# One-core two-block network: modulation products held back in stretches, score trees started one by one, input squares on ScalarE

## The chip, the cores and the metric

One core of one Trainium2 chip runs the whole program in one launch. The metric is the device time of an execution in microseconds (us), taken as the median of several runs. The engines are TensorE (PE; its weight loads are listed as PEld), VectorE (DVE), ScalarE (ACT), GpSimd (POOL) and SyncE (SP, which only issues DMAs). Each executes its own instructions in one order that is fixed before the launch.

## The reference, cut to what matters

Two networks of two layers run one after the other on a sequence of 512 vectors of width 1024, in fp32.

```python
# first network, x: 512 x 1024
x = x + even_mixer(rms(x))      # retention (4 heads) and HGRN2 (4 heads), gates, output product
x = x + memory_attention(x)     # 256 memory vectors
x = x + conv_ffn(x)
x = x + odd_mixer(rms(x))       # 8 heads of dilated attention, biases by distance
x = x + memory_attention(x)
x = x + conv_ffn(x)
# second network, context ctx: 256 x 1024
for i in range(2):
    mod = silu(c) @ ada_w[i] + ada_b[i]        # six vectors of 1024 out of 1024 x 6144 weights
    mod_c = silu(c_ctx) @ ada_w[i] + ada_b[i]
    h, hc = modulate(rms(x), mod), modulate(rms(ctx), mod_c)
    x, ctx = x + g * mixer(h, hc), ...
    x, ctx = x + g * swiglu(modulate(rms(x))), ...
out = rms(x)
```

`modulate(x, shift, scale)` is `x * (1 + scale) + shift`. The vectors `mod` and `mod_c` depend on `c`, `c_ctx` and weights alone, so that they can be computed any time before the second network needs them.

## The kernel before, in words

**Weight products.** Activations lie feature-major: 8 tiles of 128 features x 512 positions. A weight unit (128 x 1024, 512 KB) is loaded by SP into one of 4 buffers (`raw`), rounded to the matmul type by ACT (`wh`, L293), and its rest is taken by DVE (`wl`, L294). A product of one unit is 24 matmuls of 128x512 into one PSUM tile: wh by the high and the low part of the activation, and wl by the high part (`fm`, L312; `fm2_step`, L342; `fm1`, L939; `dx`, L1158; time-major forms `tm`, L357, `tm_c`, L1183, and `tm_dual`, L1202). `split` (L401 to L405) makes the two parts of an activation, with one ACT and one DVE instruction.

**Statistics.** `stat_add` squares a new tile on ACT (L423) and adds it on POOL, the last of eight on DVE (L428). `stat_end` sums over features with matmuls by a column (`colsum`, L417) and POOL takes the power -1/2 (L411). `bcast` brings the result to all partitions with four transposes on PE (L480). In the even mixer, which is the first stage, POOL both squares the eight input tiles (L513) and adds the squares (L515). `head_part` (L459, L460 on DVE) and `head_rstd` (L442 on PE) do the same for one head.

**Modulation products.** `ada(l, j)` computes vector j of layer l outside TensorE. For each of 2 halves and 8 row blocks it loads a 128x512 weight tile with SP (256 KB, L1053, two steps ahead) and adds it, scaled by one scalar per partition, to an accumulator on DVE (L1060, L1062; two instructions a step where both `mod` and `mod_c` are wanted, otherwise one). Then DVE transposes and sums (L1066, L1068), and PE adds up (L442). It is a generator: each step ends in a `yield`. The generator `side` chains all twelve vectors, with four empty turns first. `tick` advances it by one turn, and is called at the start of each weight product `fm`, `fm1`, each of `fm2_start`, and each `wt`. In layer 0 each step takes two turns, in layer 1 one. `finish_side` runs the rest at once, where the second network starts.

**Order.** The tile framework orders each engine's instructions at build time: of those it takes to be ready, it takes the one that stands first in the program, so that the program text acts as a list of priorities. `weave` writes such a text: it keeps up to `depth` generators active, takes one step of each in a round, and then runs `rate` background jobs a round.

**Stages that the change touches.** `even_mixer` projects the inputs of the HGRN2 heads (`hg_inputs`, L565 to L579), then builds the scores of four heads as trees (`tree`, L581): at each of seven levels four PE products (L591), one merge and three scalings on DVE (L609 to L622), each waiting for the level before. The trees are woven with the value products, the retention inputs and the retention heads. `odd_mixer` projects queries and keys of a head in three steps (`project`, L963) and weaves attention with the further projections and the memory keys and values of the next stage. `conv_ffn` writes its output in three passes of eight blocks; the last pass also makes the next stage's split and statistics. `ab_mixer`, the first stage of the second network, weaves the three steps of `modulate` (statistics, broadcast, the eight tiles) between the four units of the context's value product.

Of the kernel before, what the change touches and what calls it, by code (L numbers as in the profile page):

```python
# [10 lines left out]
AF = mybir.ActivationFunctionType  # L11
ALU = mybir.AluOpType
# [213 lines left out]
class Net:  # L226
    def __init__(self, ctx, tc, a):
        self.tc, self.nc, self.a = tc, tc.nc, a
        E = ctx.enter_context
        self.cp = E(tc.tile_pool(name="cp", bufs=1))  # L230
        self.xp = E(tc.tile_pool(name="xp", bufs=9))
        self.cx = E(tc.tile_pool(name="cx", bufs=9))
        self.A = E(tc.tile_pool(name="A", bufs=NSLOT))
        self.sp = E(tc.tile_pool(name="sp", bufs=40))
        self.wr = E(tc.tile_pool(name="wr", bufs=4))
        self.wh = E(tc.tile_pool(name="wh", bufs=3))
        self.wl = E(tc.tile_pool(name="wl", bufs=3))
        self.pm = E(tc.tile_pool(name="pm", bufs=4, space=PSUM))
        self.pa = E(tc.tile_pool(name="pa", bufs=4, space=PSUM))
        self.dp = E(tc.tile_pool(name="dp", bufs=1, space=bass.MemoryType.DRAM))  # L240
        self.n = 0
        self.side = None
        self.early = []
        self.consts()

# [114 lines left out]
            evac(tb, pss[tb])  # L360

    def tick(self):
        if self.side is not None and next(self.side, None) is None:
            self.side = None

    @staticmethod
    def weave(units, bg=(), depth=4, rate=1.0):

        units, bg, active, due = iter(units), iter(bg), [], 0.0
        while True:  # L370
            while len(active) < depth:
                u = next(units, None)
                if u is None:
                    break
                active.append(u)
            if not active:
                break
            for g in list(active):
                if next(g, "end") == "end":
                    active.remove(g)  # L380
            due += rate
            while due >= 1.0:
                due -= 1.0
                job = next(bg, None)
                if job is not None:
                    job()
        for job in bg:
            job()
# [115 lines left out]
    def even_mixer(self, x, filler):  # L504
        nc, a = self.nc, self.a
# [3 lines left out]
        for k in range(8):  # L509
            xs.append(self.split(x[k], scale=self.V("mixg0", k)))  # L510
            self.fm2_step(first, xs, k)
            sq = acc if k == 0 else self.T()
            nc.gpsimd.tensor_tensor(sq, x[k], x[k], ALU.mult)  # L513
            if k:
                nc.gpsimd.tensor_tensor(acc, acc, sq, ALU.add)  # L515
        first = [[ps for ps, _ in first], [self.fm("w_ev", 17, xs)]]
        rstd, _ = self.stat_end([acc])
# [9 lines left out]
        mx = self.S(4)  # L527
# [37 lines left out]
        def hg_inputs(h):  # L565
            pf, pq = first[h] if h < 2 else (self.fm("w_ev", 16 + h, xs), None)
            th = self.T()
            nc.vector.tensor_mul(th, pf, rb)
            nc.scalar.activation(th, th, AF.Tanh, scale=0.5)
            f = self.T()  # L570
            nc.vector.tensor_scalar(f, th, fa[:, h:h + 1], fb[:, h:h + 1], ALU.mult, ALU.add)
            KS = self.T()
            nc.gpsimd.tensor_scalar(KS, f, -1.0, 1.0, ALU.mult, ALU.add)
            nc.vector.tensor_scalar(f, f, 1e-6, None, ALU.max)
            if pq is None:
                pq = self.fm("w_ev", 12 + h, xs)
            QP = self.T()
            nc.vector.tensor_mul(QP, pq, rb)
            return QP, KS, f  # L579
# [128 lines left out]
            ys[h] = self.split(o)  # L708

        hv, rv, sc, ri, gates = [], [], {}, {}, {}  # L710
        inp = {0: hg_inputs(0)}
        self.mem_prep()

        def trees():
            for h in range(4):
                if h not in inp:
                    inp[h] = hg_inputs(h)
                yield tree(h, *inp[h])
# [12 lines left out]
        jobs = [next_inputs] * 3  # L731
        jobs += [lambda: self.tm("w_evt", 1, xs, v_evac(hv, False)), lambda: self.tm("w_evt", 0, xs, v_evac(rv, True))]
        jobs += [lambda: ret_in(0), lambda: ret_in(1)]
        for h in range(4):
            jobs.append(lambda h=h: retention(h, *ri[h]))
            if h < 2:
                jobs.append(lambda h=h: ret_in(h + 2))
        self.weave(trees(), jobs, depth=4, rate=0.75)
        extra = []
        jobs = iter(filler(extra))  # L740
        for h in range(8):
# [148 lines left out]
    def conv_ffn(self, l, x, st, xs, gain=None, mid=None):  # L890
        nc = self.nc
        first = self.fm2(f"w_fi{l}", (0, 22), xs)
        rstd, _ = self.stat_end(st)
        hid = []
        third = self.fm(f"w_fi{l}", 1, xs)
        rb = self.bcast_sb(rstd)

        def gate_up(j):
            pg, pu = first if j == 0 else (third if j == 1 else self.fm(f"w_fi{l}", j, xs), None)
            g, y = self.T(), self.T()  # L900
            nc.vector.tensor_mul(g, pg, rb)
            nc.scalar.activation(y, g, AF.Identity, bias=self.V(f"cb{l}", j), scale=self.V(f"cw{l}", 44 + j))
            nc.vector.scalar_tensor_tensor(y[:, 1:512], g[:, 0:511], self.V(f"cw{l}", 22 + j), y[:, 1:512], ALU.mult, ALU.add)
            nc.vector.scalar_tensor_tensor(y[:, 2:512], g[:, 0:510], self.V(f"cw{l}", j), y[:, 2:512], ALU.mult, ALU.add)
            nc.scalar.activation(y, y, AF.Gelu_apprx_tanh)  # L905
            nc.gpsimd.tensor_tensor(y, y, rb, ALU.mult)  # L906
            if pu is None:
                pu = self.fm(f"w_fi{l}", 22 + j, xs)
            nc.vector.tensor_mul(y, pu, y)
            hid.append(self.split(y))  # L910

        for p, (lo, hi) in enumerate(PARTS):
            for j in range(len(hid), min(hi + 1, 22)):
                gate_up(j)
            out, st, nxt = [], [], []
            for m in range(8):
                if mid is not None and p > 0:
                    next(mid, None)
                ps = self.fm1(f"w_fo{l}", m * 3 + p, hid[lo:hi])
                t = self.xp.tile([128, 512], F32, tag="x", name=f"x{self.n}")  # L920
                nc.vector.tensor_add(t, ps, x[m])
                out.append(t)
                if p == 2:
                    if gain is not None:
                        nxt.append(self.split(t, scale=self.V(gain, m)))
                    self.stat_add(st, m, t)
            x = out
        return x, st, nxt

    def fm1(self, w, u, xs, n=512):  # L930
# [12 lines left out]
    def odd_mixer(self, x, st, xs, filler):  # L943
# [19 lines left out]
        def project(h):  # L963
            q, k, sq, sk = self.T(), self.T(), self.T(), self.T()
            tb = self.T()
            nc.scalar.dma_start(tb, self.a["odb"][h])
            nc.gpsimd.tensor_tensor(tb, tb, odm, ALU.add)
            pk = self.fm("w_od", 8 + h, xs)
            nc.scalar.copy(k, pk)
            nc.scalar.activation(sk, pk, AF.Square)  # L970
            sk = self.head_part(sk)
            yield
            pq = self.fm("w_od", h, xs)
            nc.scalar.copy(q, pq)
            nc.scalar.activation(sq, pq, AF.Square)
            sq = self.head_part(sq)
            rk = self.head_rstd(sk, 128, xv)
            yield
            rq = self.head_rstd(sq, 128, xv)
            pb = self.bcast(rk)  # L980
            nc.vector.scalar_tensor_tensor(k, k, gqk[:, 0:1], pb, ALU.mult, ALU.mult)
            p[h] = q, k, rq, tb
# [26 lines left out]

        pj = [project(h) for h in range(8)]  # L1010
        extra = []
        for h in (0, 0, 1, 0, 1):
            next(pj[h], None)
        values(1)
        next(pj[1], None)

        def units():
            for h in range(8):
                self.run(pj[h])
                ys.append((self.T(F32R), self.T(F32R)))  # L1020
                for i in range(4):
                    yield attend(h, i, *p[h])

        jobs = [lambda h=h: next(pj[h], None) for h in range(2, 8) for _ in range(3)]
        ff = filler(extra)
        jobs = jobs[:12] + ff[:1] + jobs[12:17] + ff[1:3] + jobs[17:] + ff[3:]
        self.weave(units(), jobs, depth=3, rate=0.85)
        return self.residual("w_odo", ys, x, "xag1"), extra


# [216 lines left out]
    def ab_mixer(self, x, st, c, cs):  # L1247
# [47 lines left out]
                nc.gpsimd.tensor_tensor(t[:, 0:w], t[:, 0:w], u[:, 0:w], ALU.mult)  # L1295
                ys.append(self.split(t) if n == 4 else self.split_c(t))

        for _ in self.tm_c("w_abt", 1, cs, ev_n):
            next(mx, None)
        self.run(mx)  # L1300
        self.tm_dual("w_abt", 1, xs, None, ev_n)
        win = [[], [], [], []]
# [578 lines left out]
def body(ctx, tc, a, stop=None, start=None):  # L1881
# [32 lines left out]
    def side(ls):  # L1914
        if start in (None, "mix0"):
            for _ in range(4):
                yield True
            k.ada_prep()
        for l in ls:
            for j in range(6):  # L1920
                for _ in k.ada(l, j):
                    for _ in range(2 - l):
                        yield True

    def finish_side(l):
        while (l, 5) not in k.done:
# [76 lines left out]
```

## Time and profile before

| | |
|---|---|
| median of 3 runs | 3152.65 us (3144.85 to 3153.3) |
| the profiled execution's own time | 3151.23 us |
| its span, first to last instruction | 3149.4 us |
| PE busy | 3091.8 us, 98% of the span, 16292 matmuls |
| PEld busy | 2587.4 us, 82% |
| DVE busy | 1779.6 us, 57% |
| ACT busy | 1118.9 us, 36% |
| POOL busy | 437.8 us, 14% |
| DMA | 312.79 MB, 99 GB/s |

The shares are averages over stages with different limits. [...] A wait is the idle time of an engine before an instruction, and is put down to the instruction that ended last. Matmul ends are modelled: a matmul that is listed with 0.39 us can be followed by the next one 0.23 us after its start.

### The profile page before, as it was taken

How to read it: one execution, taken by the hardware profiler on the slowest of the kernel's cores; microseconds unless marked ns; L12 is line 12 of the kernel's file. 1: busy time of each engine (PE TensorE's matmuls, PEld its weight loads, DVE VectorE, ACT ScalarE, POOL GpSimd, SP SyncE). 2: the span in 40 equal slices, each digit the busy share in tenths (PEclk: the TensorE clock that was granted, in tenths of full speed). 3: DMA queues.
4: the chain of work that ended last, by engine and by line, in shares of the span. 5: the costliest groups of instructions: out<-in, count | busy, mean ns of one | idle time of the engine just before them, and what ended most of it. 6: DMA issues, size and time to landing. Idle time of an engine off the chain costs nothing. (4 is left out here: it accounts for less than half of the span.)

```text
span 3149.4 us, 40994 instructions
## 1 busy us (share of the span) xinstructions
PE 3091.8 (98%) x16292; PEld 2587.4 (82%) x16292; DVE 1779.6 (57%) x2894; ACT 1118.9 (36%) x1859; POOL 437.8 (14%) x375
## 2 busy tenths in 40 slices
PE   8999999999999999999999999999999999999998
PEld 6878888888877888888878778888888878888887
DVE  7867676565658767768663567343322453543333
ACT  2224353232435544423343545211212352342222
POOL 5023111010111111102021113000000320110001
PEclk9999999999999999999999999999999999999999
DMA  5224323333333423334342012332211221123222
GB/s 170 75 80 154 117 78 119 115 127 117 125 103 103 147 84 106 119 128 153 131 150 96 29 36 103 107 113 72 88 67 53 69 99 37 39 100 99 95 97 71
DMA packets 110354, 312.79 MB, mean 99 GB/s; under 512 B 12177, under 2 KB 17682, under 8 KB 110162
## 3 DMA queue, kind: packets, MB, share of 16 engines
q1 hardware_dynamic: 101968, 297.32, 28.0%
q10 hardware_dynamic: 8194, 12.86, 1.3%
q8 instruction: 128, 2.10, 0.3%
q14 instruction: 64, 0.52, 0.1%
HBM read 306.98 MB, written 3.15 MB: 98 GB/s over the span
## 5 line engine op out<-in xcount | busy, mean ns | idle before, releaser
L1158 PE MATMUL m<-t,wh 128*128 128x512 f32 (+1 forms) x4124 | 1092.1, 352 | 1.1 <-DVE t L1110 0.4
L293 ACT CAST wh<-wr 128x1024 fp32r<-128x1024 f32 (+2 forms) x485 | 488.0, 1008 | 1241.8 <-PE m L1158 419.3
L294 DVE TENSOR_TENSOR wl<-wr,wh 128x1024 fp32r<-128x1024 f32 (+2 forms) x485 | 579.3, 1195 | 453.3 <-ACT wh L293 442.0
L1158 PEld LDWEIGHTS m<-t,wh 128*128 128x128 f32 x4124 | 726.1, 190 | 114.9 <-issue 11.5
L312 PE MATMUL m<-t,wh 128*128 128x512 f32 (+1 forms) x2576 | 772.4, 382 | 0.0
L1158 PE MATMUL m<-t,wl 128*128 128x512 f32 (+1 forms) x2062 | 723.9, 351 | 0.5 <-DVE wl L294 0.5
L312 PEld LDWEIGHTS m<-t,wh 128*128 128x128 f32 x2576 | 473.9, 188 | 89.5 <-issue 1.0
L312 PE MATMUL m<-t,wl 128*128 128x512 f32 (+1 forms) x1288 | 491.1, 381 | 0.2 <-DVE wl L294 0.2
L1158 PEld LDWEIGHTS m<-t,wl 128*128 128x128 f32 x2062 | 390.6, 189 | 53.1 <-issue 1.9
L312 PEld LDWEIGHTS m<-t,wl 128*128 128x128 f32 x1288 | 242.7, 188 | 46.9 <-issue 0.7
L428 POOL TENSOR_TENSOR t<-t,t 128x512 f32<-128x512 f32 (+1 forms) x90 | 116.0, 1295 | 1163.0 <-ACT t L423 1162.7
L1062 DVE SCALAR_TENSOR_TENSOR t<-t,silc,t 128x512 f32<-128x512 f32 x280 | 219.5, 812 | 15.5 <-DMA t<-w_ada 14.9
L939 PE MATMUL m<-t,wh 128*128 128x512 f32 x704 | 217.2, 390 | 0.0
L342 PE MATMUL m<-t,wh 128*128 128x512 f32 x496 | 159.4, 401 | 7.3 <-ACT wh L293 7.3
L939 PEld LDWEIGHTS m<-t,wh 128*128 128x128 f32 x704 | 131.9, 188 | 27.2
L906 POOL TENSOR_TENSOR t<-t,t 128x512 f32<-128x512 f32 x44 | 64.8, 1473 | 549.6 <-ACT t L905 539.9
L401 ACT CAST t<-t 128x512 fp32r<-128x512 f32 x116 | 72.0, 621 | 189.6 <-DVE t L1520 104.0
L939 PE MATMUL m<-t,wl 128*128 128x512 f32 x352 | 136.9, 389 | 0.0
L1428 DVE SCALAR_TENSOR_TENSOR x<-m,modt,x 128x512 f32<-128x512 f32 (+1 forms) x70 | 49.3, 704 | 154.2 <-PE m L1158 154.2
L411 POOL TENSOR_TENSOR s<-s,nh 128x4 f32<-128x4 f32 (+2 forms) x67 | 72.3, 1081 | 429.9 <-DVE s L473 155.7
L357 PE MATMUL m<-wh,t 128*128 128x512 f32 x384 | 123.4, 397 | 0.0
L342 PEld LDWEIGHTS m<-t,wh 128*128 128x128 f32 x496 | 93.6, 192 | 26.3 <-ACT wh L293 7.3
(387 smaller groups left out, 3384.5 us busy)
## 6 DMA issues: line engine op xcount, KB each, us to landing
t<-w_ada SPq DMA_DIRECT2D x192, 256.0 KB, 4.1
wr<-w_fi SPq DMA_DIRECT2D x88, 512.0 KB, 3.3
wr<-w_gu SPq DMA_DIRECT2D x88, 512.0 KB, 3.2
wr<-w_fo SPq DMA_DIRECT2D x32, 512.0 KB, 3.4
wr<-w_dn SPq DMA_DIRECT2D x32, 512.0 KB, 3.3
wr<-w_ev SPq DMA_DIRECT2D x24, 512.0 KB, 3.2
wr<-w_xk SPq DMA_DIRECT2D x16, 512.0 KB, 3.4
wr<-w_xv SPq DMA_DIRECT2D x16, 512.0 KB, 3.2
```

The source lines that it names most:

```text
L293: nc.scalar.copy(h[:, 0:e], r[:, 0:e])
L294: nc.vector.tensor_sub(lo[:, 0:e], r[:, 0:e], h[:, 0:e])
L312: nc.tensor.matmul(ps[:, 0:n], A[:, s], B[:, 0:n], start=c == 0, stop=c == tot - 1)
L342: self.nc.tensor.matmul(ps, A[:, s], B, start=k == 0 and i == 0, stop=k == K - 1 and i == 2)
L357: nc.tensor.matmul(pss[tb], A[:, ts], B[:, s], start=(u == 0 and j == 0 and i == 0), stop=(u == nu - 1 and j == kper - 1 and i == 2))
L401: nc.scalar.copy(h[:, 0:n], src[:, 0:n])
L411: self.nc.gpsimd.tensor_tensor(r, v, self.nh[:, 0:w], ALU.pow)
L428: e.tensor_tensor(st[0][:, 0:n], st[0][:, 0:n], sq[:, 0:n], ALU.add)
L906: nc.gpsimd.tensor_tensor(y, y, rb, ALU.mult)
L939: nc.tensor.matmul(ps[:, 0:n], A[:, s], B[:, 0:n], start=c == 0, stop=c == tot - 1)
L1062: nc.vector.scalar_tensor_tensor(acc[i], r, s, acc[i], ALU.mult, ALU.add)
L1158: nc.tensor.matmul(ps[:, s], A[:, ws], B[:, s], start=j == 0 and i == 0, stop=j == last and i == 2)
```

## The change

While a new flag `quiet` is set, `tick` does nothing. It is set over the tree weave of the even mixer, over the weave of the odd mixer, and in the last pass of `conv_ffn` over the last four blocks. The layer-0 steps of `side` take one turn instead of two. `weave` gets an argument `ramp`: in round r at most 1 + r // ramp generators are active; the trees use ramp 2. The squares of the even mixer's input tiles go from POOL to ACT. The odd mixer's `project` has four steps instead of three, its key scale's sum comes a step later, and the job list and rate are fitted to that. In `ab_mixer`, `modulate` is advanced after the second and the fourth unit instead of after each.

```diff
@@ class Net, __init__
+        self.quiet = False
@@ tick
-        if self.side is not None and next(self.side, None) is None:
+        if self.side is not None and not self.quiet and next(self.side, None) is None:
             self.side = None
@@ weave
-    def weave(units, bg=(), depth=4, rate=1.0):
+    def weave(units, bg=(), depth=4, rate=1.0, ramp=None):
-        units, bg, active, due = iter(units), iter(bg), [], 0.0
+        units, bg, active, due, r = iter(units), iter(bg), [], 0.0, 0
         while True:
-            while len(active) < depth:
+            top = depth if ramp is None else min(depth, 1 + r // ramp)
+            r += 1
+            while len(active) < top:
@@ even_mixer
-            nc.gpsimd.tensor_tensor(sq, x[k], x[k], ALU.mult)
+            nc.scalar.activation(sq, x[k], AF.Square)
...
+        self.quiet = True
         inp = {0: hg_inputs(0)}
         self.mem_prep()
...
-        self.weave(trees(), jobs, depth=4, rate=0.75)
+        self.weave(trees(), jobs, depth=4, rate=0.75, ramp=2)
+        self.quiet = False
@@ conv_ffn
+                self.quiet = p == 2 and m > 3
                 ps = self.fm1(f"w_fo{l}", m * 3 + p, hid[lo:hi])
...
+        self.quiet = False
         return x, st, nxt
@@ odd_mixer, project
             sq = self.head_part(sq)
+            yield
             rk = self.head_rstd(sk, 128, xv)
-            yield
             rq = self.head_rstd(sq, 128, xv)
+            yield
             pb = self.bcast(rk)
@@ odd_mixer
-        for h in (0, 0, 1, 0, 1):
+        for h in (0, 0, 1, 0, 1, 0):
             next(pj[h], None)
         values(1)
-        next(pj[1], None)
+        for h in (1, 1):
+            next(pj[h], None)
+        self.quiet = True
...
-        jobs = [lambda h=h: next(pj[h], None) for h in range(2, 8) for _ in range(3)]
+        jobs = [lambda h=h: next(pj[h], None) for h in range(2, 8) for _ in range(4)]
         ff = filler(extra)
-        jobs = jobs[:12] + ff[:1] + jobs[12:17] + ff[1:3] + jobs[17:] + ff[3:]
-        self.weave(units(), jobs, depth=3, rate=0.85)
+        jobs = jobs[:16] + ff[:1] + jobs[16:23] + ff[1:3] + jobs[23:] + ff[3:]
+        self.weave(units(), jobs, depth=3, rate=1.05)
+        self.quiet = False
@@ ab_mixer
-        for _ in self.tm_c("w_abt", 1, cs, ev_n):
-            next(mx, None)
+        for i, _ in enumerate(self.tm_c("w_abt", 1, cs, ev_n)):
+            if i in (1, 3):
+                next(mx, None)
         self.run(mx)
@@ body, side
                 for _ in k.ada(l, j):
-                    for _ in range(2 - l):
-                        yield True
+                    yield True
```

## Rows read from the trace of the kernel before

**Rows 1.** The page's busy times: engine, busy us, share of the span, instructions.
```profile
PE 3091.8 (98%) x16292; PEld 2587.4 (82%) x16292; DVE 1779.6 (57%) x2894; ACT 1118.9 (36%) x1859; POOL 437.8 (14%) x375
```

**Rows 2.** PE's waits over the span: total us, times, longest us.
```profile
PE a L417 <- DVE t L428: 11.3, 6, 2.5
...
PE a L591 <- DVE t L578: 3.0, 1, 3.0
PE a L442 <- DVE s L460: 3.0, 3, 2.2
PE m L342 <- DVE wl L294: 2.4, 2, 1.2
...
PE a L635 <- DVE t L632: 1.3, 1, 1.3
PE a L417 <- POOL t L515: 1.2, 1, 1.2
```

**Rows 3.** Busy us (instructions) by stretch: PE, PEld, DVE, ACT, POOL; PEclk, DMA share, GB/s.
```profile
0.00:40.00 40.00, 28.97 (x108) 22.12 (x109) 27.22 (x33) 15.61 (x21) 25.87 (x20) 0.96 0.68 231
...
60.00:80.00 20.00, 16.72 (x100) 15.45 (x99) 19.39 (x37) 1.57 (x2) 1.12 (x2) 0.83 0.27 93
80.00:240.00 160.00, 158.41 (x882) 128.97 (x882) 114.20 (x225) 42.20 (x58) 25.32 (x16) 1.00 0.23 76
240.00:440.00 200.00, 197.37 (x1157) 167.06 (x1156) 142.81 (x232) 92.67 (x164) 44.95 (x33) 1.00 0.36 119
440.00:840.00 400.00, 400.00 (x1792) 330.99 (x1792) 262.88 (x337) 142.36 (x178) 53.68 (x35) 1.00 0.36 121
...
950.00:970.00 20.00, 17.82 (x103) 13.70 (x102) 15.81 (x34) 7.16 (x18) 4.50 (x4) 0.91 0.29 96
...
1600.00:1630.00 30.00, 26.35 (x106) 20.84 (x105) 22.44 (x27) 14.41 (x19) 9.86 (x6) 0.89 0.53 176
```

**Rows 4.** The instructions of lines 513, 515 and 423: duration ns min/median/max, first and last start.
```profile
L513 POOL TENSOR_TENSOR t<-xin x8: 1040/1486/2024, 4.8 to 28.1; 128x512 f32<-128x512 f32 x8
L515 POOL TENSOR_TENSOR t<-t,t x7: 1265/1627/2157, 8.7 to 30.2; 128x512 f32<-128x512 f32 x7
L423 ACT ACTIVATE t<-x x96: 400/617/635, 328.3 to 3139.1; 128x512 f32<-128x512 f32 x64, 128x256 f32<-128x256 f32 x32
```

**Rows 5.** Timeline, DVE's rest of the weights with POOL busy, then idle: start, us.
```profile
7.61 2.06 DVE L294 TENSOR_TENSOR wl<-wr,wh 128x1024 fp32r<-128x1024 f32 x1
...
54.06 1.22 DVE L294 TENSOR_TENSOR wl<-wr,wh 128x1024 fp32r<-128x1024 f32 x1
```

**Rows 6.** Timeline where the trees begin: start, us; idle time before and its releaser in brackets.
```profile
53.72 0.43 DVE L574 TENSOR_SCALAR t<-t 128x512 f32<-128x512 f32 x1 [3.98 <-POOL t L573]
...
66.15 0.74 DVE L1062 SCALAR_TENSOR_TENSOR t<-t,silc,t 128x512 f32<-128x512 f32 x1
...
67.64 2.04 PE L591 MATMUL a<-t,t 128*128 128x128 f32 x8 [2.99 <-DVE t L578]
```

**Rows 7.** Timeline in the odd mixer's weave.
```profile
956.93 2.45 DVE L1062 SCALAR_TENSOR_TENSOR t<-t,silc,t 128x512 f32<-128x512 f32 x2 [1.65 <-DMA t<-w_ada]
...
961.11 0.25 PE L442 MATMUL a<-s,fold 128*32 128x4 f32 x8 [2.18 <-DVE s L460]
```

**Rows 8.** Timeline where the second network begins.
```profile
1605.58 2.57 DVE L1062 SCALAR_TENSOR_TENSOR t<-t,silc,t 128x512 f32<-128x512 f32 x2
...
1610.36 1.80 PE L417 MATMUL a<-c,t 128*128 128x1 f32 x8 [2.48 <-DVE t L428]
...
1617.26 0.60 PE L480 MATMUL a<-ident,s 128*128 128x128 f32 x4
...
1624.90 0.50 PE L1202 MATMUL m<-wh,t 128*128 128x512 f32 x1 [1.10 <-DVE t L1110]
```

**Rows 9.** DVE's waits for the modulation weights: total us, times, longest us.
```profile
DVE t L1062 <- DMA t<-w_ada: 14.9, 13, 4.3
```

**Rows 10.** Line 1062 alone by stretch: DVE busy us (instructions), PEclk, DMA share, GB/s.
```profile
240.00:440.00 200.00, 21.23 (x28) 1.00 0.36 119
440.00:840.00 400.00, 50.67 (x66) 1.00 0.36 121
```

More of the change, by code (lines that the diff above doesn't have):

```diff
@@ L976, in project @@
             sq = self.head_part(sq)
+            yield
             rk = self.head_rstd(sk, 128, xv)
+            rq = self.head_rstd(sq, 128, xv)
             yield
-            rq = self.head_rstd(sq, 128, xv)
             pb = self.bcast(rk)
```

## The prediction

> **What bounds the kernel now.** First the page's busy times: PE is busy for 98% of the span, DVE for 57% [rows 1]. The 440 to 840 us stretch shows what that means: PE without a gap, 1792 matmuls in 400 us, 223 ns each, and so 24 x 0.223 = 5.4 us for one weight unit [rows 3]. The change takes no matmul away. All that it can win is PE's idle time, 3149.4 - 3091.8 = 57.6 us, and what PE loses while its clock is granted at 0.5. So I read second PE's waits [rows 2], then the stretches around the edits with their clock [rows 3], and last the timeline at each wait [rows 5 to 8]. The reader is to see there that after a wait of 2 to 3 us the clock falls for some microseconds: 0.83 over 60 to 80 us, 0.91 over 950 to 970, 0.89 over 1600 to 1630, against 1.00 in stretches without such a wait [rows 3]. A stretch loses about (1 - PEclk) x its length on top of the wait.
>
> **Input squares by ACT.** POOL does 8 squares of 1.49 us and 7 additions of 1.63 us, the last starting at 30.2 us [rows 4], and PE then waits 1.2 us for the sum [rows 2]. Without the squares POOL has 7 x 1.63 = 11.4 us left, so the sum is done before PE has finished its three products: this wait goes. DVE also gains. Its rest of a weight unit took 2.06 us beside POOL and 1.22 alone [rows 5], and PE waited 2 x 1.2 us for just these two instructions [rows 2]; 0.84 us less in each saves 1.7 of 2.4 us, of which I count 1.5. The mean clock of the first 40 us, 0.96, is 1.6 us lost [rows 3]; I count half as won, 0.8. ACT gets 8 x 0.62 = 4.9 us [rows 4] and has 40 - 15.6 = 24.4 us free in that stretch [rows 3]; the work is hidden unless the squares are put ahead of the splits that PE waits for, where each costs up to 0.62 us. Sum 1.2 + 1.5 + 0.8 = **3.5 us won**, bounds -4.9 (every square in the way) and 1.2 + 2.4 + 1.6 = 5.2.
> [...]
>
> **Trees.** At 64.65 us PE waits 3.0 us for the last head's inputs (L578), behind a DVE that has stood 3.98 us for POOL and then did modulation products [rows 6]. With its clock the stretch loses 3.0 + 0.17 x 20 = 6.4 us [rows 3]; from 80 to 240 us another 1.6 us are idle, 1.3 of them at L635 [rows 2, 3]. The text before makes all four heads' inputs before the first tree step, and rounds 1 to 3 then hold only empty jobs. With ramp 2 the trees begin in rounds 0, 2, 4 and 6, so heads 2 and 3 are projected (four units, 21 us of PE) while trees 0 and 1 run; the weave has 17 rounds instead of 11, so all but one of its 13 jobs stand beside trees. The 12 units in it no longer tick: 6 steps, some 9 us of DVE at two times 0.75 us [rows 6], leave the one stage where DVE works 114.2 of 160 us and 19.4 of 20 [rows 3]. POOL, free sooner, has the memory's squares done before the heads' keys need it. What is late next is the last tree alone: its levels follow one another with less beside them. I leave one wait like L635's, 1.3 us, and 1.2 for it: 8.0 - 2.5 = **5.5 us won**, bounds -3 (a wait like L578's comes back in a second place) and 8.0.
>
> **Odd mixer.** PE's 2.2 us wait for L460 came of DVE's order: DVE stood 1.65 us for a modulation tile, did two products in 2.45 us, and only then the head's sums [rows 7]. With the clock, 0.09 x 20 = 1.8, that is 4.0 us [rows 3]. Quiet takes those products out, and the extra step puts a weight unit (5.4 us) between a head's sums and the matmul that needs them. The job list keeps pace: 24 + 15 jobs at 1.05 a round are 37 rounds, 18 + 15 at 0.85 were 39. Small waits in the same weave may give 0.5. **4.5 us won**, bounds 0 and 4.8.
>
> **Start of the second network.** The last residual block's sum was held up on DVE by two products of 2.57 us, and PE waited 2.48 us [rows 8]. Quiet alone takes that away, and the statistics standing after the second context unit (2.7 us later) cover it twice. With the clock, 0.11 x 30 = 3.3, the loss is 5.8, plus 1.1 at the first product that reads the modulated tiles: 6.9 us. But the broadcast now stands behind the fourth unit. Before, it began at 1617.26 and PE could pass its last wait at 1624.90, 7.6 us later, with 5.5 us of context units between [rows 8]. Now nothing lies between. Bounds for the new wait: the same chain, 7.6 - 0.6 = 7.0 us, or, with DVE and ACT free, the broadcast's followers alone, some 3 to 4 us (two DVE, two ACT instructions and one of POOL, 0.6 to 1.5 each, by the kinds in [rows 4 to 6]). The clock then falls as after the other waits, 1.8 to 3.4. I take 4 + 2.4 = 6.4: **0.5 us won**, bounds 6.9 - 10.4 = -3.5 and 6.9 - 4.8 = 2.1. The quiet end of the first conv_ffn has no wait of note: 0.
>
> **Denser products elsewhere.** Turns before: 4 + 192 + 96; now 4 + 96 + 96. Units that tick: 28 in the first stage (24 after the trees, 4 ahead of them), 16, 64, 12, 16, 64, together 200, so all vectors are ready when the first network ends, layer 0 after 104 units. Before, layer 0 needed most of the second conv_ffn and layer 1 reached into the second network; there DVE is relieved, where it bounds nothing: 0. In 440 to 840 us there were 66 products in 50.7 us [rows 10]; now about 64 steps of two, 128, so +62 x 0.77 = 48 us, and some 10 for four more halves' transposes. DVE goes from 262.9 to about 320 of 400 us [rows 3, 10], 80%, hidden behind PE by weights prepared up to three units ahead. From 240 to 440 us there are 28 products [rows 10], 48 with each unit ticking: +15 us on 142.8 of 200 [rows 3]. The tiles are loaded two steps ahead, which is now two units (11 us) instead of four. DVE waited 14.9 us for them in 13 places [rows 9], and of these PE felt the one in rows 7. I count **1.5 us lost**, bounds 0 and 24 (six waits such as that one, 4.0 each).
>
> **Sum.** 3.5 + 5.5 + 4.5 + 0.5 - 1.5 = 12.5 us. The profiled execution took 3151.2 us, near the 3152.7 median of the runs, so I subtract from 3151.2: **3139 us**, 0.4% less. A measurement of this kernel can tell 0.3%, 9.5 us, from no change; faster means below about 3143.
>
> **The rivals.**
> *The waits only move.* For: the broadcast without cover is plain in the text; the trees' last levels have little beside them. Then the second network's start gives -3.5, the trees 2, the rest as above: 3.5 + 2 + 4.5 - 3.5 - 1.5 = 5, 3146 us, no change. Against: the two units behind the old broadcast did not prevent the old wait either, so the chain has slack to lose. Chance 0.26.
> *Denser products bind DVE.* DVE executes in order, so that each late modulation tile or POOL instruction holds up the weights' rests behind it. The place is 240 to 440 us and the first conv_ffn's last pass, where products, splits and POOL's additions meet; the price is 4.0 us a wait; from the fourth wait on (14 + 1.5 against 4 x 4.0) the gain is gone, and at six it is 3151.2 - 14 + 24 = 3161 us, slower. For: half the lead for the tiles. Against: 80% load and three units of stock. Chance 0.10.
> *All touched waits vanish*, at the upper bounds: 5.2 + 8.0 + 4.8 + 2.1 = 20, 3131 us. The second start speaks against it. Chance 0.10.
>
> **How the numbers follow.** The forecast has 0.54, with a range of its own from 3132 to 3147 (each term half way to its bounds), of which about 0.45 lie below 3143. Faster: 0.45 + 0.10 = 0.55. Within 0.3%: 0.09 + 0.25 = 0.34. Slower: 0.11. The range for 8 in 10 takes in the moved waits whole and most of the high gain: 3125 to 3155.
>
> **What would show it.** In the new profile: no wait at L342 for wl above 0.5 us and none at L417 for POOL; no wait of 3 us at L591, PEclk 1.00 over the trees; no wait at L442 in the odd weave, and no L1062 there; at the second network's start no wait at L417 but one of 3 us or more at L1202 or at the tiles' makers; no L1062 after the first network. Wrong would be new waits of over 2 us between 240 and 840 us, or an L1062 ahead of a late L294 there; or a PE as idle as before with the waits at other lines.

## The result, and the profile after

The changed kernel takes 3166.28 us (median of 5 runs, 3164.23 to 3168.97) against 3149.13 of the kernel before on the same chip: ratio 1.0061, interval 1.0050 to 1.0073 (that of the two medians is 1.0054). It is slower by 17 us; the forecast was 3139 us. The profiled execution of after took 3168.89 us, its span 3167.1, so that the spans of before and after (3149.4) differ by 17.7 us. In after.py the lines stand 1 to 12 lines lower: L294 is now L295, L312 L313, L405 L409, L442 L446, L591 L595, L939 L947, L1062 L1074, L1202 L1214.

First the page's busy times of after, to be read beside [rows 1]:

```profile
PE 3097.7 (98%) x16292; PEld 2588.0 (82%) x16292; DVE 1781.4 (56%) x2894; ACT 1121.4 (35%) x1867; POOL 423.9 (13%) x367
```

PE has the same 16292 matmuls. It idles 69.4 us instead of 57.6, and its matmuls take 5.9 us more: the loss is new waits and the clock behind them. Where it lies is read from the first and last start of lines that mark the ends of stages (view of one line; first and last start are the two numbers ahead of the forms). Before:

```profile
L648 PE MATMUL a<-t,t x32: 272/275/275, 213.5 to 240.4; 128*128 128x128 f32 x32
L939 PE MATMUL m<-t,wh x704: 387/389/499, 577.7 to 1604.5; 128*128 128x512 f32 x176
```

After, the same two lines (the trees' last outputs; the products of `conv_ffn`'s last pass in both blocks):

```profile
L652 PE MATMUL a<-t,t x32: 272/275/275, 214.3 to 243.0; 128*128 128x128 f32 x32
L947 PE MATMUL m<-t,wh x704: 387/389/502, 598.0 to 1627.5; 128*128 128x512 f32 x176
```

With the first score of the odd mixer (908.4 before, 932.0 after) and the first product of the modulated tiles (1623.2, 1643.5) the span falls into six stretches:

| stretch | before | after | won | forecast |
|---|---|---|---|---|
| start to the last tree output | 240.4 | 243.0 | -2.6 | 3.5 + 5.5 |
| to the first product of the first `conv_ffn`'s last pass | 337.3 | 355.0 | -17.7 | -1.5 for these two |
| to the odd mixer's first score | 330.7 | 334.0 | -3.3 | |
| to the second `conv_ffn`'s last product | 696.1 | 695.5 | 0.6 | 4.5 |
| to the first product of the modulated tiles | 18.7 | 16.0 | 2.7 | 0.5 |
| to the end | 1526.2 | 1523.6 | 2.6 | 0 |

The second row is as large as the whole loss; the others cancel. That stretch by itself, before (PE, PEld, DVE, ACT, POOL busy us and instructions; PEclk, which is the mean granted TensorE clock as a share of full speed, DMA share, GB/s, as in [rows 3]):

```profile
240.43:577.74 337.31, 334.68 (x1779) 280.65 (x1778) 239.25 (x358) 148.39 (x238) 69.48 (x49) 1.00 0.36 120
```

After, with two pieces of it:

```profile
460.00:475.00 15.00, 11.80 (x40) 8.96 (x39) 12.69 (x16) 3.69 (x6) 3.51 (x2) 0.77 0.37 123
540.00:555.00 15.00, 11.25 (x50) 8.81 (x50) 13.10 (x21) 4.36 (x6) 1.48 (x1) 0.89 0.49 170
242.98:598.01 355.03, 342.35 (x1788) 285.46 (x1786) 276.92 (x416) 147.71 (x237) 67.42 (x48) 0.98 0.39 132
```

PE idled 2.6 us there before and idles 12.7 now; the clock, 0.98 of 355 us, gives about 7: 10.1 + 7.1 = 17.2 of the 17.7 us. DVE has 37.7 us more to do and is still only 78% busy, but 13.10 of 15 us around one of the waits. Line 1074 alone, by stretch, beside [rows 10] (instructions 28 to 47, 66 to 126, as forecast):

```profile
240.00:440.00 200.00, 35.57 (x47) 0.99 0.41 138
440.00:840.00 400.00, 94.00 (x126) 0.99 0.39 133
```

PE's waits between 240 and 840 us, after. In the same window the kernel before has 2.5 us of them, 1.8 of these at L480:

```profile
PE m L313 <- DVE wl L295: 4.7, 4, 3.1
PE a L446 <- DVE t L1080: 3.7, 1, 3.7
PE a L446 <- DVE s L464: 2.1, 2, 1.8
PE a L484 <- POOL s L415: 1.5, 1, 1.5
```

The two longest, in the timeline (start, us, instruction, in brackets the idle time before it and its releaser). The wait for a weight unit's rest:

```profile
452.62 2.00 ACT L294 CAST wh<-wr 128x1024 fp32r<-128x1024 f32 x2 [1.46 <-PE m L343]
...
454.52 0.88 DVE L1072 TENSOR_SCALAR t<-t,silc 128x512 f32<-128x512 f32 x2
455.31 1.41 DVE L1074 SCALAR_TENSOR_TENSOR t<-t,silc,t 128x512 f32<-128x512 f32 x2
456.64 0.74 DVE L409 SCALAR_TENSOR_TENSOR t<-x,vec,t 128x512 fp32r<-128x512 f32 x1
457.30 1.78 DVE L1074 SCALAR_TENSOR_TENSOR t<-t,silc,t 128x512 f32<-128x512 f32 x1
459.01 0.74 DVE L409 SCALAR_TENSOR_TENSOR t<-x,vec,t 128x512 fp32r<-128x512 f32 x1
459.18 1.86 PE L313 MATMUL m<-t,wh 128*128 128x512 f32 x6
459.20 1.05 ACT L294 CAST wh<-wr 128x1024 fp32r<-128x1024 f32 x1 [2.30 <-issue]
459.67 0.74 DVE L1074 SCALAR_TENSOR_TENSOR t<-t,silc,t 128x512 f32<-128x512 f32 x1
460.33 0.68 DVE L500 TENSOR_TENSOR x<-m,x 128x512 f32<-128x512 f32 x1
460.93 1.40 DVE L1074 SCALAR_TENSOR_TENSOR t<-t,silc,t 128x512 f32<-128x512 f32 x2
462.25 0.74 DVE L409 SCALAR_TENSOR_TENSOR t<-x,vec,t 128x512 fp32r<-128x512 f32 x1
462.92 1.21 DVE L295 TENSOR_TENSOR wl<-wr,wh 128x1024 fp32r<-128x1024 f32 x1
464.18 0.79 PE L313 MATMUL m<-t,wl 128*128 128x512 f32 x1 [3.14 <-DVE wl L295]
```

The same place in before:

```profile
444.62 2.01 ACT L293 CAST wh<-wr 128x1024 fp32r<-128x1024 f32 x2 [1.33 <-PE m L342]
...
446.25 1.22 DVE L294 TENSOR_TENSOR wl<-wr,wh 128x1024 fp32r<-128x1024 f32 x1
```

Three units are cast in after, the first by 453.68 us, the second by 454.62, the third by 460.25, and PE does the first two matmuls of each (x6 at 459.18), which read only high parts. Counted in order (485 casts, 485 rests), the rest at 462.92 is that of the first unit: DVE reaches it 9.2 us after its cast. In between DVE is never idle; eight modulation products (L1072, L1074) take 0.88 + 1.41 + 1.78 + 0.74 + 1.40 = 6.2 us, and residuals, splits and two small instructions take what remains. In before the first rest begins 0.6 us after its cast (446.25 and 445.67). High parts are thus in stock and rests are not: when the first cast was ready, PE had one unit with its rest to do, until 459.1 us. One product took 1.78 us beside a POOL addition (456.98 to 458.54), 1.0 more than the next. Behind the wait PEclk is 0.50 in each microsecond from 464 to 469 and 1.00 in each from 470 to 476, 0.77 on the mean of 15 us; three matmuls take 1.29 us there at 0.50 (starts 464.77 to 466.06) and 0.69 at 1.00 (470.60 to 471.29). In before, behind the wait of [rows 6], PEclk is 0.50 in each microsecond from 68 to 74. The wait for the modulation's own fold:

```profile
541.36 1.22 DVE L295 TENSOR_TENSOR wl<-wr,wh 128x1024 fp32r<-128x1024 f32 x1
...
543.76 0.69 DVE L915 TENSOR_TENSOR t<-m,t 128x512 f32<-128x512 f32 x1 [1.18 <-POOL t L912]
...
545.14 0.69 DVE L406 TENSOR_TENSOR t<-t,t 128x512 fp32r<-128x512 f32 x1 [0.68 <-ACT t L405]
545.74 1.30 DVE L1078 STREAM_TRANSPOSE t<-t 128x512 f32<-128x512 f32 x2
546.97 1.24 DVE L1080 TENSOR_REDUCE t<-t 128x16 f32<-128x512 f32 x2
...
548.26 0.26 PE L446 MATMUL a<-t,fold 128*32 128x16 f32 x8 [3.75 <-DVE t L1080]
```

Eight matmuls of 0.26 us in all stand in PE's order ahead of a weight unit whose rest has been there since 542.6 us. What they read is made last by a DVE that has the block's convolution to do first, and stands in it 1.2 us for POOL and 0.7 for ACT.

The first stage. DVE and POOL at the start of after:

```profile
8.90 0.74 DVE L409 SCALAR_TENSOR_TENSOR t<-xin,vec,t 128x512 fp32r<-128x512 f32 x1
...
10.38 12.50 POOL L519 TENSOR_TENSOR t<-t,t 128x512 f32<-128x512 f32 x7 [9.94 <-ACT t L517]
10.95 8.58 DVE L409 SCALAR_TENSOR_TENSOR t<-xin,vec,t 128x512 fp32r<-128x512 f32 x5
...
19.45 2.30 DVE L295 TENSOR_TENSOR wl<-wr,wh 128x1024 fp32r<-128x1024 f32 x1
...
23.48 0.50 PE L343 MATMUL m<-t,wh 128*128 128x512 f32 x1 [2.24 <-DVE t L409]
```

POOL is done at 22.9 instead of 31.5, but its seven additions now follow one another, and five splits beside them take 1.72 us each instead of 0.74; in before six splits beside POOL's squares and additions took 9.51 us, 1.59 each. The two waits for wl [rows 2] have become one of 2.24 us for the last split, which stands behind a rest of 2.30 us, and one of 0.34 for a wl. And the trees of after:

```profile
50.91 0.62 POOL L577 TENSOR_SCALAR t<-t 128x512 f32<-128x512 f32 x1
51.56 0.43 DVE L578 TENSOR_SCALAR t<-t 128x512 f32<-128x512 f32 x1 [2.67 <-POOL t L577]
...
52.47 2.85 PE L595 MATMUL a<-t,t 128*128 128x128 f32 x16 [3.23 <-DVE t L623]
```

It is the wait of [rows 6] again, 3.2 us instead of 3.0 and 15 us earlier: POOL squares and adds the memory's tiles until 50.9 us and so comes late to L577, DVE waits for it, a tree's scaling (L623) stands behind it, and PE behind that. The clock falls there too, 0.91 over 40 to 60 us (1.00 before).

### The profile page after: what moved, and what is told of

It reads as the page before. It is cut to its first block, busy times and chain, and to the rows that moved or that the text cites. A ratio compares the mean times of both kernels' runs of the same rounds, so it can differ in the third digit from the quotient of the medians.

```text
span 3167.1 us, 40970 instructions
## 1 busy us (share of the span) xinstructions
PE 3097.7 (98%) x16292; PEld 2588.0 (82%) x16292; DVE 1781.4 (56%) x2894; ACT 1121.4 (35%) x1867; POOL 423.9 (13%) x367
## 3 DMA queue, kind: packets, MB, share of 16 engines
HBM read 306.98 MB, written 3.15 MB: 98 GB/s over the span
## 5 line engine op out<-in xcount | busy, mean ns | idle before, releaser
L294 ACT CAST wh<-wr 128x1024 fp32r<-128x1024 f32 (+2 forms) x485 | 488.0, 1008 | 1254.7 <-PE m L1170 421.9
L295 DVE TENSOR_TENSOR wl<-wr,wh 128x1024 fp32r<-128x1024 f32 (+2 forms) x485 | 578.1, 1193 | 471.4 <-ACT wh L294 459.6
L313 PE MATMUL m<-t,wh 128*128 128x512 f32 (+1 forms) x2576 | 778.6, 384 | 0.2
L313 PEld LDWEIGHTS m<-t,wh 128*128 128x128 f32 x2576 | 476.9, 190 | 92.0 <-issue 1.4
L313 PE MATMUL m<-t,wl 128*128 128x512 f32 (+1 forms) x1288 | 493.5, 384 | 5.1 <-DVE wl L295 5.1
L313 PEld LDWEIGHTS m<-t,wl 128*128 128x128 f32 x1288 | 244.1, 190 | 53.0 <-DVE wl L295 6.7
L1074 DVE SCALAR_TENSOR_TENSOR t<-t,silc,t 128x512 f32<-128x512 f32 x280 | 214.5, 799 | 10.9 <-DMA t<-w_ada 10.4
L947 PE MATMUL m<-t,wh 128*128 128x512 f32 x704 | 217.7, 390 | 0.7 <-ACT t L405 0.4
L947 PEld LDWEIGHTS m<-t,wh 128*128 128x128 f32 x704 | 131.8, 188 | 28.6 <-ACT t L405 0.8
L405 ACT CAST t<-t 128x512 fp32r<-128x512 f32 x116 | 72.0, 621 | 202.4 <-DVE t L1533 104.0
L947 PE MATMUL m<-t,wl 128*128 128x512 f32 x352 | 137.0, 389 | 0.0
L343 PEld LDWEIGHTS m<-t,wh 128*128 128x128 f32 x496 | 93.1, 190 | 30.2 <-ACT wh L294 7.7
```

The lines of the kernel that those rows point to most:

```text
L294: nc.scalar.copy(h[:, 0:e], r[:, 0:e])
L295: nc.vector.tensor_sub(lo[:, 0:e], r[:, 0:e], h[:, 0:e])
L313: nc.tensor.matmul(ps[:, 0:n], A[:, s], B[:, 0:n], start=c == 0, stop=c == tot - 1)
L343: self.nc.tensor.matmul(ps, A[:, s], B, start=k == 0 and i == 0, stop=k == K - 1 and i == 2)
L405: nc.scalar.copy(h[:, 0:n], src[:, 0:n])
L947: nc.tensor.matmul(ps[:, 0:n], A[:, s], B[:, 0:n], start=c == 0, stop=c == tot - 1)
```

## The experiments

The theory at the start: one turn a step makes DVE's in-order products stand ahead of what PE needs. Its rivals: the quiet stretches or the new orders cost the time; the products' loads do; the ramp and the late broadcast do. Beside the experiments the kernel before had medians of 3147.2, 3148.3 and 3148.7 us, so that medians of different experiments can be compared to about 2 us.

**Two turns, no quiet** (all else as after).

```diff
-        if self.side is not None and not self.quiet and next(self.side, None) is None:
+        if self.side is not None and next(self.side, None) is None:
...
-                    yield True
+                    for _ in range(2 - l):
+                        yield True
```

> The changed kernel with layer 0's steps taking two turns again and the quiet flag without effect, so that the modulation products are as thin as before and run everywhere; squares on ScalarE, ramp, the odd mixer's steps and the later broadcast stay. Theory 1 (dense products hold up VectorE, which executes in order): the two waits of 3 to 4 us in 450 to 550 us and the waits at L313 for wl in 240 to 480 us go; of the 17 us lost about 20 come back, while the quiet in the odd mixer and the trees is given up (some 4): 3148 to 3153 us. Theory 2 (the new order of the first stage and of the odd mixer is what costs): stays at 3162 to 3168.

3149.89 us, ratio to before 1.0006 (0.9997 to 1.0016). The stretch from the last tree output to the last pass's first product:

```profile
244.93:581.98 337.05, 334.44 (x1779) 280.64 (x1778) 239.26 (x358) 148.50 (x238) 69.36 (x49) 1.00 0.36 120
```

This is the row of before to 0.3 us. The loss is thus in the turns or in quiet; squares, ramp, odd order and broadcast together leave the time as it was (they lose 4.5 us up to the last tree output).

**One turn alone** (the kernel before with this edit).

```diff
-                    for _ in range(2 - l):
-                        yield True
+                    yield True
```

> The kernel before with one edit alone: layer 0's steps take one turn instead of two. Theory 1: new PE waits of 2 to 4 us between 240 and 840 us with falls of the clock, 3166 to 3174 us. Theory 2: about 3149, within 4 us.

3178.94 us, 1.0097 (1.0083 to 1.0111): alone it costs 32 us by the medians, more than expected and more than the whole change, whose other parts, with the quiet stretches, take some of it back. PE's waits between 240 and 840 us:

```profile
PE a L442 <- DVE t L1068: 6.7, 2, 5.6
PE a L480 <- POOL s L411: 6.5, 4, 3.8
```

The 5.6 us are a fold at 572.5 us, the 3.8 us a broadcast at 268.1.

**One turn without the loads, and without most products** (two kernels, each from the one before). In the first, each half loads one weight tile and uses it eight times; in the second, the steps k = 1 to 6 load their tile and compute nothing. The modulation vectors are not the reference's in either.

```diff
@@ without loads
-                if k < 6:
+                if k == -2:
...
-                r = ahead.pop(0)
+                r = ahead[0]
@@ without products
-                    else:
+                    elif k == 7:
```

> As e2 (before, with one turn a step), but each half of a modulation vector loads its first weight tile alone and uses it for all eight steps, so that seven of eight loads are left out and the vectors have other values; VectorE's work is the same. If VectorE's own work in order is what costs: 3165 to 3180, waits of over 2 us at the fold matmuls (L442) and power (L411) between 240 and 600 us as in e2. If late weight tiles are what holds VectorE up: 3145 to 3155.

> As e2, but all weight tiles are loaded and only the first and the last step of each half are computed on VectorE (the vectors have other values). If VectorE's work costs: 3135 to 3147, no wait of over 2 us between 240 and 600 us. If the denser DMAs on SyncE's queue cost by themselves: 3165 or more.

Without loads 3171.93 us (1.0071, 1.0057 to 1.0085), without products 3137.70 us (0.9966, 0.9954 to 0.9979). Over the whole program the loads take 7 of the 32 us with them, three quarters of the products all of them and 10 more. Not so in the stretch from the last tree output to the last pass's first product, 337.3 us in before. With one turn alone and without products (without loads it is 360.2 us):

```profile
244.10:607.10 363.00, 343.31 (x1795) 286.04 (x1794) 280.23 (x426) 148.22 (x238) 71.39 (x49) 0.97 0.39 131
234.20:578.60 344.40, 336.62 (x1796) 282.42 (x1795) 221.04 (x342) 148.23 (x238) 66.94 (x49) 1.00 0.40 138
```

Of the 25.7 us lost here 2.8 go with the loads and 18.6 with the products; 7.1 stay without the products. PE's waits between 240 and 840 us then begin with

```profile
PE a L480 <- POOL s L411: 4.1, 2, 2.8
```

So most of the loss is DVE's time for the products and little of it the transfers. Against what was expected, one wait of over 2 us remains, for POOL's power; what makes it late was not told apart. The rest of the gain lies elsewhere: the last tree output comes at 234.2 us instead of 240.4, and the first product of the modulated tiles follows the second `conv_ffn` 5.7 us sooner than in before. At the old pace, then, the products were not free either.

**One turn, the fold a turn later.** In `ada`, ahead of the fold's matmuls, from the kernel with one turn alone:

```diff
+        yield True
```

> As e2 (before, with one turn a step), but ada yields one turn more between the last sums on VectorE and the fold matmuls on PE. In e2 PE stood 1.1, 5.6 and 2.6 us at those folds (L442 behind L1068), and the clock fell after two of them. Theory: PE's wait came from its own fold in its order, not from late weights; the three waits go, with their clock some 12 us: 3164 to 3170 us against e2's 3179. Rival (VectorE is simply late there, so PE waits at the next weight rest or power): 3174 or more, with waits at L312 or L411 in their place.

3160.67 us, 1.0039 (1.0025 to 1.0053): 18 us less than with one turn alone, more than expected. PE's waits between 240 and 840 us begin now with

```profile
PE m L312 <- DVE wl L294: 6.5, 4, 3.4
```

The folds' waits are gone from there, and waits for rests have come in their place: two ways in which the same products reach PE. The last tree output is 2.7 us later than with one turn alone (246.8, 244.1), so that the 18 us come from the stretches behind, 10 of them from the next one (363.0 us with one turn alone, 353.0 here).

**The first stage: its order undone; the ramp alone undone; the memory's squares later** (each from after).

```diff
@@ order undone
-            nc.scalar.activation(sq, x[k], AF.Square)
+            nc.gpsimd.tensor_tensor(sq, x[k], x[k], ALU.mult)
@@ order undone, and squares without ramp
-        self.weave(trees(), jobs, depth=4, rate=0.75, ramp=2)
+        self.weave(trees(), jobs, depth=4, rate=0.75)
@@ ramp, memory squares later: moved behind the weave of the trees
-        self.mem_prep()
...
+        self.mem_prep()
```

> The changed kernel with the input squares back on GpSimd and the trees without ramp; still quiet over the trees and one turn a step. From the two traces the stretch up to the last tree output took 2.5 us longer after the change, so both edits together win nothing. Theory 1: 3162 to 3168, the waits of 450 to 550 us remain. Theory 2: about 3150.

> The changed kernel with the trees' ramp alone undone: against e3 it differs in the input squares on ScalarE alone. In e3 the last tree output stood at 235.2 us, in the changed kernel at 243.0, so squares and ramp together lose 7.8. Theory ramp (trees begun early meet VectorE and GpSimd at the head inputs): about 3155 to 3160, last tree output at 232 to 236. Theory squares (additions back to back on GpSimd slow VectorE while PE needs its splits): 3160 to 3168, last tree output at 240 to 244 and the wait of 2.2 us at 21 us still there.

> The changed kernel with the memory's loads and squares (mem_prep) put behind the tree weave, ramp kept. In the changed kernel the second head's keys on GpSimd stood behind the memory squares, VectorE behind the keys (2.7 us), and PE behind the first tree's scaling (3.2 us). Theory: that wait goes, the last tree output moves from 243.0 to about 236 to 239, 3160 to 3163 us. Rival (the ramp costs because a tree alone gives each engine too little between its levels): the waits of the first tree remain, 3165 or more.

3160.51 us (1.0035, 1.0022 to 1.0049), 3155.98 (1.0021, 1.0012 to 1.0031) and 3161.68 (1.0039, 1.0025 to 1.0053). The first is a little below theory 1's range; its longest waits between 240 and 840 us are those of after (3.1 and 3.7 us). The trees' last outputs, without the ramp:

```profile
L652 PE MATMUL a<-t,t x32: 272/275/276, 205.6 to 233.9; 128*128 128x128 f32 x32
```

and with it, the memory's squares later:

```profile
L652 PE MATMUL a<-t,t x32: 273/275/275, 208.4 to 238.1; 128*128 128x128 f32 x32
```

Against 243.0 of after the ramp costs 9.1 us, and 4.9 of these go with the POOL work that stood ahead of L577: the 3.2 us wait is gone, and PEclk over 40 to 60 us is 1.00 instead of 0.91. What the other 4.2 us are was not told apart. With the order undone the last output comes at 235.2, so that quiet over the trees wins 240.4 - 235.2 = 5.2 us by itself up to there (its products then come later), and the squares on ACT 1.3.

**The old broadcast** (from after).

```diff
-        for i, _ in enumerate(self.tm_c("w_abt", 1, cs, ev_n)):
-            if i in (1, 3):
-                next(mx, None)
+        for _ in self.tm_c("w_abt", 1, cs, ev_n):
+            next(mx, None)
```

> The changed kernel with the broadcast after the second context unit again (modulate advanced after every unit). In all runs with the later broadcast the context's four units and what follows up to the first product of the modulated tiles took 15.6 us, in e2, which has no modulation products there, 12.5. Theory: the quiet end of conv_ffn alone takes the wait at the sum away and the later broadcast costs 3.1: about 3162 to 3164 us against 3166, the wait at L1214 down to 1.3. Rival (the later statistics are what removes the wait): a wait of 2 us or more at L421 comes back, 3166 or more.

3161.95 us, 1.0043 (1.0029 to 1.0057), some 4 us less than after. The wait at the modulated tiles' first product:

```profile
PE m L1214 <- DVE t L1122: 1.3, 1, 1.3
```

With the late broadcast it is this row of after, and the clock over 1640 to 1650 us is 0.83:

```profile
PE m L1214 <- ACT t L1115: 3.1, 1, 3.1
```

From the first context product to the first product of the modulated tiles it is 12.5 us instead of 15.6 (before: 18.2). The wait for the last residual sum does not come back: quiet alone had removed it.

**Late edits with thin products; the parts that win; density in `conv_ffn` only.** The first is after with the first stage as before, trees not quiet, and two turns except at every fifth step. The second keeps quiet over the trees, the odd weave and the second `conv_ffn`'s end, takes the old broadcast, squares by POOL, no ramp, and the same thin pace. The third is the second with one turn inside both `conv_ffn`, two elsewhere, and the fold a turn later.

```diff
@@ thin pace, both
-                for _ in k.ada(l, j):
+                for n, _ in enumerate(k.ada(l, j)):
                     yield True
+                    if l == 0 and n % 5:
+                        yield True
@@ the first
-        self.quiet = True
...
@@ the second
-                self.quiet = p == 2 and m > 3
+                self.quiet = l == 1 and p == 2 and m > 3
...
@@ the third, in place of the thin pace
                     yield True
+                    if l == 0 and not k.dense:
+                        yield True
...
```

> The first stage as before (squares on GpSimd, no ramp, trees not quiet) and layer 0's steps take two turns except every fifth step, which takes one; the odd mixer's steps and quiet, the quiet end of both conv_ffn and the later broadcast as changed. From the two traces the odd mixer took 8.1 us less after the change and the start of the second network 2.6 less, none of it owed to the pace. Theory 1: 3136 to 3142 us, no wait over 1 us between 440 and 840. Theory 2 (odd mixer's order costs too): 3150 or more.

> A candidate: quiet over trees and odd weave, odd mixer's four steps, quiet end of the second conv_ffn alone; squares on GpSimd, no ramp, broadcast after the second context unit as before, two turns a step in layer 0 except every fifth. From the traces so far: first stage -5 (e3), odd mixer with what follows -3, second start -5.5 (as in e2, which has no products there), against before's 3147 to 3149; some 1 to 3 lost where every fifth step is dense: 3134 to 3140. If the late broadcast helps rather than costs, no better than 3140.

> As e10, but one turn a step inside both conv_ffn (where each unit leaves VectorE the most time) and two turns elsewhere in layer 0, and the fold one turn later as in e11. Theory: first network as e10 or 1 us less, since the one dense wait left in e10 (2.0 us at 1270) was a fold; more of layer 1 is done by the end of the first network, so the waits of 1.6 and 2.9 us at 1923 and 1930 us shrink towards one of 2.3: 3132 to 3139 us. Rival (density costs in conv_ffn as well): 3142 or more, waits between 440 and 840 us.

The first, 3154.37 us (1.0023, 1.0014 to 1.0032), missed what was expected: with the trees not quiet the wait of [rows 6] is still there (3.4 us at L595 at 63 us), the late broadcast costs 3.1 us at L1213, and even at the thin pace PE waits 2.0 us for a fold at 518 us. The second is the best kernel of the case: 3140.79 us, 0.9973 (0.9962 to 0.9984), 7.5 us below before and 0.8 above the range that was expected. Its longest wait between 240 and 840 us is one of 1.5 us for POOL's power, and its last tree output is at 233.8. The third, 3141.85 us (0.9985, 0.9974 to 0.9996), missed too: the density won nothing, and a fold is late again, by 3.9 us at 555 us, so a fold one turn later was not late enough there.

## Why the prediction was wrong

The step that failed is "Denser products elsewhere", counted as 1.5 us lost between bounds of 0 and 24. It measured 21.0 (17.7 + 3.3), near the far bound, and the rival "Denser products bind DVE" at 3161 us, with a chance of 0.10, was the mechanism. The counts in that step were nearly right: 173 products where 176 were forecast, DVE 304 of 400 us where 320 were. What failed is the conclusion that DVE at 80% is hidden "by weights prepared up to three units ahead". A mean share says nothing of the ten microseconds in which products, splits and a rest come together; at 460 us three units had their high parts, none of them its rest, and DVE had had 9.2 us of other work ahead of the first. The loads, of which the step's loss was made (six late tiles), carry 7 of the 32 us of this edit alone. The rival's place was partly right: waits of 1.5 and 1.8 us stand at 264 and 282 us, inside it, the two longest at 461 and 545 us between its two halves. Its price of 4.0 us a wait was low for the long ones, 3.1 + 0.23 x 15 = 6.6 and 3.7 + 0.11 x 15 = 5.4, and high for the two short ones (3.3 + 0.06 x 30 = 5.1 for both, by PEclk 0.94 over 260 to 290 us); together 17.1 of the 17.7 us. And it looked for rests alone: the folds, PE's own instructions for the modulation, wait 3.7 us where the rests wait 4.7. Two slips in the sums change nothing: the gain without this step is 14, not 14 + 1.5, and layer 0's turns are 4 + 96 = 100, not 104.

**Squares by ACT**, 3.5: 1.3 us by the last tree output (one profiled execution each). PE's wait for the sum is gone as said; the saving on DVE was spent by the additions, which moved together instead of going away. PEclk over the first 40 us is 1.00 in after, but with the same squares and no ramp 0.96, as in before, so that the 0.8 us of the clock are not the squares' either.

**Trees**, 5.5: quiet alone wins 5.2, so that part stands. The ramp, for which the term left 2.5 us, costs 9.1. The step saw that the last tree would be alone. It failed where it has POOL done with the memory's squares before the heads' keys need it: they last until 50.9 us, with a head's keys (L577) behind them.

**Odd mixer**, 4.5. The wait of [rows 7] is gone and the weave shorter, 144.1 to 136.0 us (first to last score). But from the odd mixer's first score to the second `conv_ffn`'s last product only 0.6 us are won. The two parts of that stretch, parted at the last score, before and after:

```profile
908.40:1052.50 144.10, 140.76 (x903) 115.90 (x902) 110.20 (x252) 75.53 (x186) 28.31 (x24) 0.99 0.31 104
1052.50:1604.80 552.30, 550.98 (x2622) 456.64 (x2621) 390.95 (x560) 214.70 (x319) 87.41 (x62) 1.00 0.37 126
932.00:1068.00 136.00, 134.72 (x869) 111.84 (x868) 94.95 (x230) 72.21 (x183) 27.01 (x24) 1.00 0.28 91
1068.00:1627.70 559.70, 555.29 (x2662) 459.41 (x2661) 378.04 (x534) 215.71 (x320) 88.15 (x63) 1.00 0.39 131
```

Of the 8.1 us by which the weave is shorter, 6.0 are busy time of PE, with 34 matmuls fewer, more than one weight unit; behind it stand 4.3 us of busy time and 40 matmuls more. So most of the shorter weave is work moved behind it. The 2.1 us of idle time that go from the weave come back as 3.1 us behind it (1.3 to 4.4), 1.4 of them at a fold at 1334 us.

**Start of the second network**, 0.5: 2.7 won, above its upper bound of 2.1; up to the last of the 240 products of the modulated tiles, behind the fall of the clock, it is 2.5. The new wait is where it was forecast, 3.15 us against 4, and its clock 1.7 against 2.4. The late broadcast is the wrong half: the old one wins 3.1 us more.

**To the end**, 0: 2.6. Between after and the kernel with the old broadcast, whose text from there on is the same, this stretch differs by 7 us, so it is left unexplained.

Of the signs named ahead, those of being wrong, "new waits of over 2 us between 240 and 840 us, or an L1062 ahead of a late L294 there" came true in both halves; of those of being right, "no wait of 3 us at L591" did not.

## What to carry to other kernels

Background work on an in-order engine is priced by what stands behind each piece, not by that engine's mean share: here DVE, 78% busy with 37.7 us more to do, began a rest 9.2 us after its cast, behind eight products, and let 17.7 us through to PE. Look for the nearest consumer that the bound engine waits for (a weight's rest, a fold), and ask how long before its need it becomes ready. And measure a change by stretches between the same lines: a 9 us loss and a 5 us gain in one stage were told apart by one start time.

## What the runs showed of the hardware

Beside seven POOL additions back to back (12.50 us, 1.79 each) five DVE splits of two inputs took 8.58 us, 1.72 each, instead of 0.74, and the rest of a unit took 2.30 instead of 1.22: 0.98 and 1.08 us lost. An addition with DVE idle beside it took 1.26 us ([rows 4], the last of L515, at 30.2 us), so that the 1.79 are 0.53 longer. One addition and one split together took about 1.7 us, where one after the other they would take, by the times alone, 1.26 + 0.74 = 2.00.
